# Layer 1's memory projections behind the modulation, other places for weight halves, and unread transposes of the identity on TensorE

## The chip, the cores and the metric

The kernel runs on one core of a Trainium2 chip. What is measured is the device time of one execution in microseconds (us). A core has five engines that run side by side, each with its own queue of instructions in a fixed order: TensorE (PE; its weight loads are listed apart, as PEld), VectorE (DVE), ScalarE (ACT), GpSimd (POOL) and SyncE (SP), which here issues the transfers from memory. An instruction waits on semaphores for its inputs and for free buffers, and everything behind it on its engine waits with it.

## The reference

One sequence of 256 tokens, 1024 wide, in float32, goes through two blocks.

The first block has two layers. For each, `mod = silu(c) @ ada_w[layer] + ada_b[layer]` gives six rows (shift, scale and gate, twice), and then

```python
h = rms_norm(x, norm1_g) * (1 + sc1) + sh1
x = x + g1 * mixer(h)                  # layer 0: retention and attention; layer 1: stick-breaking
h = rms_norm(x, norm2_g) * (1 + sc2) + sh2
x = x + g2 * grouped_moe(h, ...)       # 16 experts, two for each token
```

`grouped_moe` takes a sigmoid score of each token for each expert, picks the best of four groups of experts, two experts in it, and adds their SwiGLU results with the scores as weights.

The second block has two layers too: half a feed-forward network, a mixer (layer 0: the RWKV scan; layer 1: dilated attention on shared keys and values) and another half network. Both mixers also attend to a memory of 256 rows, `mem`, whose keys and values for layer l are `rms_norm(mem, mem_norm[l]) @ mem_w_kv[l]`, with a norm on each head of the keys.

## The kernel before

**Layout and products.** The tokens stand transposed, `xT` [128, 8, 256]: eight tiles of 128 features by 256 tokens. Weights come in pieces of [128, 2048], 1 MB each, by SyncE's transfers (L300 and the loads beside it), into a few rooms that are used in turn. For most products each operand is split into a rounded part (`wh`, `xh`, by ScalarE, L350) and a remainder (`wl`, `xl`, by VectorE or GpSimd, L351), and TensorE multiplies three pairs (`mm3`). Every matmul is recorded at L330 and every transpose by the identity at L346. A transpose of the identity itself gives nothing that is used; such an instruction is called a turn here, as is any use of `tr`.

**What sets the order.** The program is written as one sequence, function after function. A planner then orders the instructions of each engine: of those that are ready by its own modelled durations it takes the one that the program has first. `tc.issue_after(instruction)` holds what stands under it until that instruction has been issued. RWKV_ORDER (L203) and B_ORDER (L204) are orders of steps written out by hand. Buffers with a tag (`self.t`, `self.ps` for the banks in which matmuls accumulate) are used in turn, so an instruction can also wait for a room.

**Start.** `first_layer` (L1149) for layer 0 first calls `mem_kv` (L1243): the memory is loaded (one transfer), its squares are summed (`prep`, `step`, `fin`), it is scaled by each layer's norm gain, and the keys and values for both layers are projected, 32 matmuls for each of the keys and values of a layer. Then the modulation rows are made from `ada` weights (1 MB each), the norm of x is finished (`fin`, L411: a reciprocal root, two transposes that spread it to `rB`), and `modulated` (L427) makes the mixer's input. For each of eight tiles VectorE multiplies by `rB`, multiplies by the gain and adds the shift, and subtracts the rounded part that ScalarE makes. The first weight of the mixer is split ahead of all that, by `ws` (L309).

**Layer 1's entry.** The same `fin` and `modulated` run once layer 0's experts have been added to x.

**Routing and experts.** `residual` (L462) adds the mixer's output to x. `route` (L815) makes the routing logits: eight matmuls of a broadcast shift, then the token's own, on a bank `g`. `moe` (L1061) turns the input (sixteen transposes, `hY`), waits for VectorE to pick the experts, and gathers the tokens of each by matmuls with one-hot matrices (`gather`, 32 for a pair of experts). The experts are done in eight blocks of two experts by 64 tokens (a block that depends on the data follows for more tokens). `hidden` (L1013) and `down` (L1033) run the matmuls of the two experts in turn, expert 0 on the upper 64 columns of TensorE and expert 1 on the lower, each with its own weight piece: four halves of gate and up and two of down in a block. `scatter` (L1055) adds the results into four banks; at the end VectorE adds these to x and the next norm's sums are taken.

**The second block.** `rwkv` (L1283, its loop over RWKV_ORDER at L1579) and `b_mixer` (L1601, loop at L1621) run the steps of the two mixers; the feed-forward networks are before and after them.

Of the kernel before, what the change touches and what calls it, by code (L numbers as in the profile page):

```python
# [199 lines left out]
F32R = mybir.dt.float32r  # L200
RWKV_LANES = 3
RWKV_BANKS = dict(pp=1, g0=(1, 1), g1=(1, 1), l0=2, l1=2, l2=2)
RWKV_ORDER = "M s0 M M M s1 s2 p0 s3 m0 p1 s4 s5 p2 m1 s6 m2 s7 s8 p3 p4 s9 a3 a0 m3 m4 a1 p5 m5"  # L203
B_ORDER = "n q2 n q1 q2 M0 q0 q1 M1 q0 P1 P0"  # L204
B_OUT = 1, 0
B_BANKS = dict(pp=2, tn=1, a0=2, a1=2, x=1)
SHARED_ORDER = "012345"
# [33 lines left out]
class Net:  # L241
# [67 lines left out]
    def ws(self, name, i):  # L309

        if (name, i, "split") in self.ahead:
            return self.ahead.pop((name, i, "split"))
        t = self.ahead.pop((name, i), None)
        if t is None:
            t = self.raw(name, i)
        o = []
        for h in range(2):
            hi, lo = (self.tile([128, 1024], n, F32R, 3) for n in ("wh", "wl"))
            self.split(t[:, 1024 * h:1024 * h + 1024], hi, lo, self.lo_engines[self.nlo % len(self.lo_engines)])
            self.nlo += 1  # L320
            o.append((hi, lo))
        return o

    def v(self, name):
        s, w = VEC[name]
# [17 lines left out]

    def tr(self, out, x):
        p = x.shape[0]
        self.nc.tensor.transpose(out, x, self.ident[:p, :p])  # L346

    def split(self, src, hi, lo, eng=None):

# [74 lines left out]
        st.rB = self.tile([128, 256], "rB", bufs=2)  # L424
        nc.scalar.activation(st.rB, p.rearrange("p t z -> p (t z)"), AF.Copy)

    def modulated(self, st, gain, shift):  # L427

        nc = self.nc
        x = self.xtiles()  # L430
# [31 lines left out]
    def residual(self, name, mix, chunks, banks, after, gate=None):  # L462

        xT = self.xT
        p = [self.ps(b, [128, 2, 256]) for b in banks]
        n = len(chunks)
        for i, c in enumerate(chunks):
            w = self.ws(name, c)
            if i < n - 1:
                order = [(h, d) for h in range(2) for d in range(8)]  # L470
            else:
                order = [(h, d) for d in (0, 2, 4, 6, 1, 3, 5, 7) for h in range(2)]
            for h, d in order:
                self.mm3(p[d // 2][:, d % 2], [y[:, d * 128:d * 128 + 128] for y in w[h]], mix[2 * c + h],
                         i == h == 0 and d % 2 == 0, i == n - 1 and h == 1)
# [339 lines left out]
    def route(self, st, gain, shift):  # L815
# [197 lines left out]
    def hidden(self, xg, wsrc):  # L1013

        nc = self.nc
        V = nc.vector
        gu = []
        for nm in ("eg", "eu"):
            p = self.ps("g")
            for h in range(2):  # L1020
                w = [wsrc(nm, e, h) for e in range(2)]
                for k in range(4):
                    for e in range(2):
                        kk = 4 * h + k
                        self.mm(p[64 * e:64 * e + 64], xg[kk][:, 64 * e:64 * e + 64], w[e](k), kk == 0, kk == 7)
            gu.append(p)
        th = self.t("th", [128, 512])
        nc.scalar.activation(th, gu[0], AF.Tanh, scale=0.5)
        V.scalar_tensor_tensor(th, th, 1.0, gu[0], op0=OP.add, op1=OP.mult)
        V.tensor_tensor(th, th, gu[1], op=OP.mult)  # L1030
        return th

    def down(self, th, wsrc, wc):  # L1033

        nc = self.nc
        V = nc.vector
        p = self.ps("x", [128, 4, 128])
        for f in range(4):
            self.tr(p[:, f], th[:, f * 128:f * 128 + 128])
        hT = self.t("heT", [128, 4, 128])  # L1040
        nc.scalar.activation(hT, p, AF.Copy)
        out = []
        for n in range(2):
            w = [wsrc("ed", e, n) for e in range(2)]
            p = self.ps("g")
            for f in range(4):
                for e in range(2):
                    self.mm(p[64 * e:64 * e + 64], hT[:, f, 64 * e:64 * e + 64], w[e](f), f == 0, f == 3)
            hi, lo = self.t("yh", [128, 512], F32R), self.t("yl", [128, 512], F32R)
            nc.scalar.activation(hi, p, AF.Copy, scale=wc)  # L1050
            V.scalar_tensor_tensor(lo, p, wc, hi.bitcast(F32), op0=OP.mult, op1=OP.subtract)  # L1051
            out.append((hi, lo))
        return out

    def scatter(self, y, sc, acc, first, last):  # L1055
        for d in range(8):
            c = d % 4 * 128
            for part in range(2):
                self.mm(acc[d // 2][:, d % 2], y[d // 4][part][:, c:c + 128], sc, first and d % 2 == part == 0, last and part == 1)

    def moe(self, l, st, after, ahead):  # L1061
        nc = self.nc
# [6 lines left out]
        for t in range(2):  # L1069
            h = []  # L1070
            for half in range(2):
                p = self.ps("acc", [128, 512])
                with self.tc.issue_after(st.last.ins):
                    for k in range(4):
                        self.tr(p[:, 128 * k:128 * k + 128], xT[:, 4 * half + k, t * 128:t * 128 + 128])
# [66 lines left out]
        self.wturn = 0  # L1142
        for key in ahead:
            self.ahead[key] = self.raw(*key)
        for d in range(8):
            V.scalar_tensor_tensor(xT[:, d], acc[d // 2][:, d % 2], gate[:, d:d + 1], xT[:, d], op0=OP.mult, op1=OP.add)
            after(d)

    def first_layer(self, l, st, nxt):  # L1149
        nc = self.nc  # L1150
        xT = self.xT
        if l == 0:
            self.use(A=dict(cb=4, dec=2, rope=1, rq=1, rk=1, rv=1, rg=1, av=2, hn=2, hsq=1, q=2, k=2, sT=2, Pa0=1, Pa1=1, PTa0=1, PTa1=1,
                            me0=(4, 4), me1=(8, 4), me2=(18, 4), me3=(22, 4)),
                     B=dict(ra=2, rb=2, nx=8), C=dict(oa0=1, oa1=1), P=EVEN_BANKS)
            self.mem_kv()
            for k in range(0, 8, 2):
                nc.sync.dma_start(xT[:, k:k + 2], self.a["xT"].rearrange("p (k t) -> p k t", k=8)[:, k:k + 2])
            for d in range(8):
# [5 lines left out]
                     C=dict(neg1=1, one=1, never=1),  # L1165
                     P=ODD_BANKS)
        st = st()
        self.fin(st, "tn" if l == 0 else "o")
        V, P = self.nc.vector, self.nc.gpsimd
        self.lo_engines = [dict(V=V, P=P)[c] for c in LO_FIRST[l]]  # L1170
        key = (("even_i", dict(g0=8, g1=11, h0=0, h1=1)[EVEN_ORDER[:2]]), ("odd_i", 0))[l]
        self.ahead[(*key, "split")] = self.ws(*key)
        x = self.modulated(st, self.mod_gain(l, 1, self.v(f"n1_{l}")), self.mod[l][:, 0:8])
        mix = self.mixed()
        if l == 0:
            jobs = iter(ADA0)
# [63 lines left out]
            V.scalar_tensor_tensor(xT[:, d], p[:, 0], 0.25, xT[:, d], op0=OP.mult, op1=OP.add)  # L1240
            after(d)

    def mem_kv(self):  # L1243

        nc = self.nc
        mT, other = (self.tile([128, 8, 256], n) for n in ("ml", "mh"))
        self.load(mT, self.a["memT"].rearrange("p (k t) -> p k t", k=8))
        ws = [[self.wload(self.a[f"memkv{l}"][i], f"me{2 * l + i}") for i in range(2)] for l in range(2)]
        st = self.prep("ad", late=7)
        for d in range(8):  # L1250
            self.step(st, d, mT[:, d])
            for l, to in enumerate((other, mT)):
                nc.scalar.activation(to[:, d], mT[:, d], AF.Copy, scale=self.v(f"memn{l}")[:, d:d + 1])
        st = st()
        self.fin(st, "ad", False)
        self.kv = self.tile([128, 2, 4, 256], "kv")
        for l, x in enumerate((other, mT)):
            ps = []
            for i, w in enumerate(ws[l]):
                p = self.ps(f"a{i}", [128, 2, 256])  # L1260
                for t in range(2):
                    for k in range(8):
                        self.mm(p[:, t], x[:, k, t * 128:t * 128 + 128], w(k // 2)[:, k % 2 * 256:k % 2 * 256 + 256], t == k == 0, k == 7)
                ps.append(p)
            kT, v = self.kv[:, l, :2], self.kv[:, l, 2:]
            k = self.head_norm(ps[0], st.r)
            for t in range(2):
                nc.scalar.activation(v[:, t], ps[1][:, t], AF.Copy, scale=st.r[:, t:t + 1])
            self.memory[l] = kT, v
            self.channels(k, self.v(f"memk{l}"), kT)  # L1270

    def gain8(self, name):
        g = self.t("g8", [128, 1])
# [9 lines left out]
    def rwkv(self, st, mix, partial, memory, tags):  # L1283
# [317 lines left out]
    def b_mixer(self, st, dkv, kv, after):  # L1601
# [17 lines left out]
        q = [o[:, i] for o in o3 for i in range(2)]  # L1619
        normed = {}  # L1620
        for what in B_ORDER.split():  # L1621
            if what[0] in "nq":
                c = 0 if what == "n" else 1 + int(what[1])
                if c not in normed:
# [104 lines left out]
```

## Time and profile before

| | |
|---|---|
| median of the runs | 2148.67 us (2148.67, 2152.56, 2137.82) |
| the profiled execution | 2150.5 us, its span 2148.7 us |
| mean granted clock of TensorE | 0.965 of full |
| busy: PE | 2025.2 us (94% of the span) |
| busy: PEld | 1517.2 us |
| busy: DVE | 1143.9 us |
| busy: ACT | 854.1 us |
| busy: POOL | 478.9 us |
| transfers | 481.71 MB, 224 GB/s on average |

The span is the time from the first to the last instruction of the profiled execution; what lies around it is 1.8 us. TensorE's busy share is over the whole span and holds stretches of different kinds. All times below count from the span's start. In rows, `p<-wh,B` reads: into a bank `p` from the tiles `wh` and `B` by the program's names; PEclk is the clock that TensorE was granted in the stretch, 1.00 for 2.4 GHz and 0.50 for 1.2 GHz. The stages in order: memory and modulation to 67 us, the even mixer to 223, routing to 247, layer 0's experts to 535, the entry of layer 1 to 555, the odd mixer to 702, routing to 722, layer 1's experts to 975, then the second block with the scan mixer from 1170 and the last mixer from 1866 us.

### The profile page before, as it was taken

What the parts mean: (1) busy time and instruction counts of PE and PEld (TensorE: products, weight loads), DVE (VectorE), ACT (ScalarE), POOL (GpSimd) and SP (SyncE); (2) the same over time, 40 slices, a digit from 0 to 9 for tenths busy, and PEclk for the clock granted to TensorE, in tenths of its full rate; (3) what the DMA queues carried; (4) which work ended last, traced back from release to release, by engine and by line L of the source; (5) the groups of instructions that cost most, each with busy time, mean ns of one, the idle gap of its engine ahead of it and who ended that gap; (6) DMA issues with size and microseconds to landing.
All of it is one profiled execution on the core that took longest, in us unless ns stands there. A gap on an engine that the chain in (4) does not pass through costs nothing.

```text
span 2148.7 us, 32734 instructions
## 1 busy us (share of the span) xinstructions
PE 2025.2 (94%) x12766; PEld 1517.2 (71%) x12766; DVE 1143.9 (53%) x2331; ACT 854.1 (40%) x1566; POOL 478.9 (22%) x501
## 2 busy tenths in 40 slices
PE   8999999689899999799999899989999999899999
PEld 6778644233767544337888787768889888888887
DVE  2756511121533511207776778767767676746774
ACT  3443311102444321015554434335555555445652
POOL 1001100000000100003533443225523453422540
PEclk9999899999899999999999999989999999988999
DMA  9779599879377599793552221025555555512553
GB/s 373 290 262 367 210 421 425 354 313 391 123 282 275 226 416 424 308 416 138 186 187 98 106 83 44 21 83 192 185 188 176 177 195 180 204 59 98 195 183 114
DMA packets 80899, 481.71 MB, mean 224 GB/s; under 512 B 8800, under 2 KB 12384, under 8 KB 29792
## 3 DMA queue, kind: packets, MB, share of 16 engines
q1 hardware_dynamic: 80736, 479.52, 58.4%
q8 instruction: 105, 1.72, 0.3%
q14 instruction: 58, 0.48, 0.1%
HBM read 478.43 MB, written 1.05 MB: 223 GB/s over the span
## 4 chain that ended last, share of the span: by engine, by line
PE 51%; DVE 5%; issue 1%; ACT 1%; POOL 1%; DMA 0%; DVEq 0%; ACTq 0%; POOLq 0%
PE p L330 50%; PE p L346 1%; DVE wl L351 1%; DVE s_hsum L522 0%; DVE A L1430 0%; DVE B L1403 0%; DMA w<-a_o 0%; DVE A L1481 0%; ACT wh L350 0%; POOL acc L401 0%; DVE s_hsum L514 0%; DVE w L1503 0%; DVE s_rs_oh L361 0%; DVE C L1555 0%; DVE s_rs_th L362 0%
## 5 line engine op out<-in xcount | busy, mean ns | idle before, releaser
L351 DVE TENSOR_TENSOR wl<-w,wh 128x1024 fp32r<-128x1024 f32 x352 | 454.0, 1291 | 223.0 <-ACT wh L350 219.9
L350 ACT ACTIVATE wh<-w 128x1024 fp32r<-128x1024 f32 x384 | 404.8, 1057 | 347.9 <-PE p L330 321.8
L330 PE MATMUL p<-xh,wh 128*128 128x512 f32 (+1 forms) x1056 | 328.3, 366 | 10.2 <-ACT xh L350 4.1
L330 PE MATMUL p<-xl,wh 128*128 128x512 f32 (+1 forms) x1056 | 320.1, 359 | 0.0
L330 PE MATMUL p<-xh,wl 128*128 128x256 f32 x880 | 251.4, 286 | 1.2 <-DVE wl L351 1.2
L330 PE MATMUL p<-xl,wl 128*128 128x256 f32 x880 | 248.8, 283 | 0.0
L330 PEld LDWEIGHTS p<-xh,wh 128*128 128x128 f32 x1056 | 191.5, 193 | 50.1 <-issue 5.9
L330 PEld LDWEIGHTS p<-xl,wh 128*128 128x128 f32 x1056 | 187.0, 188 | 37.1 <-issue 5.5
L330 PEld LDWEIGHTS p<-xh,wl 128*128 128x128 f32 x880 | 168.0, 191 | 3.1 <-DVE wl L351 1.6
L330 PEld LDWEIGHTS p<-xl,wl 128*128 128x128 f32 x880 | 165.1, 188 | 1.8 <-issue 1.4
L330 PE MATMUL p<-A,wh 128*128 128x512 f32 x448 | 159.4, 397 | 0.0
L401 POOL TENSOR_TENSOR acc<-acc,sq 128x256 f32<-128x256 f32 x44 | 44.0, 1000 | 409.3 <-ACT sq L396 407.8
L330 PEld LDWEIGHTS p<-B,A 128*128 128x128 f32 x706 | 92.2, 196 | 60.9 <-issue 39.5
L330 PE MATMUL p<-A,wl 128*128 128x256 f32 x448 | 125.8, 281 | 0.0
L330 PE MATMUL p<-B,A 128*128 128x256 f32 (+1 forms) x706 | 114.4, 305 | 9.5 <-DVE A L1051 2.3
L351 POOL TENSOR_TENSOR A<-B,A 128x256 fp32r<-128x256 f32 x56 | 82.8, 1478 | 140.3 <-ACT A L350 140.1
L1051 DVE SCALAR_TENSOR_TENSOR A<-p,s_wc,A 128x512 fp32r<-128x512 f32 x34 | 25.5, 751 | 157.7 <-ACT A L1050 146.9
L330 PE MATMUL p<-w,B 128*64 128x512 f32 x256 | 109.1, 616 | 0.0
L330 PE MATMUL p<-wh,B 128*128 128x256 f32 (+1 forms) x312 | 96.8, 417 | 11.6 <-PEq L1133 11.6
L330 PE MATMUL p<-A,A 64*64 64x64 f32 (+8 forms) x868 | 102.1, 286 | 5.0 <-DVE A L1541 3.0
L330 PEld LDWEIGHTS p<-A,wh 128*128 128x128 f32 x448 | 84.2, 188 | 20.3
L351 POOL TENSOR_TENSOR wl<-w,wh 128x1024 fp32r<-128x1024 f32 x32 | 77.4, 2417 | 90.9 <-ACT wh L350 90.7
(459 smaller groups left out, 3991.3 us busy)
## 6 DMA issues: line engine op xcount, KB each, us to landing
w<-fprei SPq DMA_DIRECT2D x44, 1024.0 KB, 4.8
w<-fposti SPq DMA_DIRECT2D x44, 1024.0 KB, 4.8
wa<-ada SPq DMA_DIRECT2D x42, 1024.0 KB, 6.4
w<-ed SPq DMA_DIRECT2D x24, 1024.0 KB, 12.8
w<-eg SPq DMA_DIRECT2D x22, 1024.0 KB, 13.4
w<-fpreo SPq DMA_DIRECT2D x22, 1024.0 KB, 4.8
w<-fposto SPq DMA_DIRECT2D x22, 1024.0 KB, 4.8
wa<-ed SPq DMA_DIRECT2D x16, 1024.0 KB, 12.6
```

The lines of the kernel that those rows point to most:

```text
L330: return self.nc.tensor.matmul(out, lhsT, rhs, start=start, stop=stop, skip_group_check=True, **k)
L346: self.nc.tensor.transpose(out, x, self.ident[:p, :p])
L350: self.nc.scalar.activation(hi, src, AF.Copy)
L351: (eng or self.nc.vector).tensor_tensor(lo, src, hi.bitcast(F32), op=OP.subtract)
L401: nc.gpsimd.tensor_tensor(st.acc, st.acc, sq, op=OP.add)
L1051: V.scalar_tensor_tensor(lo, p, wc, hi.bitcast(F32), op0=OP.mult, op1=OP.subtract)
```

## The change

It has four parts.

1. `mem_kv` is cut in two: `mem_load` (the loads, the squares and the scaling; the memory comes in four transfers, not one) and `mem_kv(l)`. Layer 0's part stands where both stood; layer 1's part comes after `modulated`. The memory's norm is finished behind layer 0's projections.
2. `modulated` splits the two halves of the mixer's first weight behind tiles 0 and 3, not ahead of all. In layer 0 the eight multiplications by `rB` stand ahead of the rest. In layer 1 a tile takes two three-operand instructions on VectorE and one on ScalarE between them, which adds the shift as a bias.
3. Turns that nobody reads (`warm`) stand at eight places: 6 in `route`, behind the residual's last matmul, and 14 in `moe`, behind the turns of the input (both in both layers); 6 in `moe` behind the last `scatter` (both layers); 6 and 10 around layer 1's `fin`; 8 in `rwkv` ("W" in its order) and 12 in `b_mixer`.
4. In `hidden` and `down` the matmul of expert 1 comes ahead of that of expert 0.

```diff
-RWKV_ORDER = "M s0 M M M s1 s2 p0 ...
-B_ORDER = "n q2 n q1 q2 M0 q0 q1 M1 q0 P1 P0"
+RWKV_ORDER = "M s0 W M M M s1 s2 p0 ...
+B_ORDER = "n q2 W n q1 q2 M0 q0 q1 M1 q0 P1 P0"
...
+    def warm(self, n, bank):
+        p = self.ps(bank, [128, 128]) if isinstance(bank, str) else bank
+        for _ in range(n):
+            self.tr(p, self.ident)
...
-    def modulated(self, st, gain, shift):
+    def modulated(self, st, gain, shift, key, early):
         x = self.xtiles()
+        halves = self.halves(*key)
+        o = []
+        ts = []
+        for k in range(8):
+            ts.append(self.t("nx", [128, 256]))
+            if early:
+                V.tensor_tensor(ts[k], self.xT[:, k], st.rB, op=OP.mult)
         for k in range(8):
             hi, lo = x[k]
-            t = self.t("nx", [128, 256])
-            nc.vector.tensor_tensor(t, self.xT[:, k], st.rB, op=OP.mult)
-            nc.vector.tensor_scalar(t, t, gain[:, k:k + 1], shift[:, k:k + 1], op0=OP.mult, op1=OP.add)
-            self.split(t, hi, lo)
+            t = ts[k]
+            if early:
+                V.tensor_scalar(t, t, gain[:, k:k + 1], shift[:, k:k + 1], op0=OP.mult, op1=OP.add)
+                self.split(t, hi, lo)
+            else:
+                V.scalar_tensor_tensor(t, self.xT[:, k], gain[:, k:k + 1], st.rB, op0=OP.mult, op1=OP.mult)
+                nc.scalar.activation(hi, t, AF.Identity, bias=shift[:, k:k + 1])
+                V.scalar_tensor_tensor(lo, t, shift[:, k:k + 1], hi.bitcast(F32), op0=OP.add, op1=OP.subtract)
+            if k in (0, 3):
+                o.append(next(halves))
+        self.ahead[(*key, "split")] = o
         return x
...
     # route
-        p = self.ps("g", [128, 16])
+        p = self.ps("g")
+        with self.tc.issue_after(self.last.ins):
+            self.warm(6, p[:, 128:256])
+        p = p[:, :16]
...
     # hidden and down
-                    for e in range(2):
+                    for e in (1, 0):
...
     # moe, behind the sixteen turns of the input
+        with self.tc.issue_after(turn.ins):
+            self.warm(14, "x")
...
     # moe, behind the last scatter
+        with self.tc.issue_after(self.last.ins):
+            self.warm(6, "x")
...
     # first_layer
-            self.mem_kv()
+            self.mem_load()
+            self.mem_kv(0)
...
-        self.fin(st, "tn" if l == 0 else "o")
+        for n in (6, 10):
+            if l:
+                with self.tc.issue_after(st.last.ins):
+                    self.warm(n, "o")
+            self.fin(st, "tn" if l == 0 else "o")
...
-        self.ahead[(*key, "split")] = self.ws(*key)
-        x = self.modulated(st, self.mod_gain(l, 1, self.v(f"n1_{l}")), self.mod[l][:, 0:8])
+        x = self.modulated(st, self.mod_gain(l, 1, self.v(f"n1_{l}")), self.mod[l][:, 0:8], key, l == 0)
+        if l == 0:
+            self.mem_kv(1)
...
-    def mem_kv(self):
+    def mem_load(self):
-        self.load(mT, self.a["memT"].rearrange("p (k t) -> p k t", k=8))
+        for k in range(0, 8, 2):
+            self.load(mT[:, k:k + 2], self.a["memT"].rearrange("p (k t) -> p k t", k=8)[:, k:k + 2])
...
+    def mem_kv(self, l):
+        st, xs, ws = self.mem
+        x = xs[l]
...
+        if l == 0:
+            self.fin(st, "ad", False)
...
     # rwkv ("l2", 8) and b_mixer ("x", 12)
+            if what == "W":
+                with self.tc.issue_after(self.last.ins):
+                    self.warm(8, "l2")
+                continue
```

`halves` is the loop of `ws` as a generator: it makes one half of a weight's split each time it is asked. `fin` returns at once when the norm's row is there, so its second call in layer 1 does nothing.

## Rows read from the trace of the kernel before

**Rows 1.** Stretches: from:to, length, busy (x instructions) PE PEld DVE ACT POOL, PEclk, DMA, GB/s
```profile
66.60:223.30 156.70, 156.51 (x1232) 128.55 (x1229) 93.59 (x223) 62.94 (x111) 11.86 (x14) 1.00 0.81 307
...
974.80:982.20 7.40, 5.50 (x19) 4.82 (x19) 6.72 (x12) 5.05 (x11) 0.00 (x0) 0.54 0.31 102
...
1180.20:1187.00 6.80, 3.91 (x20) 3.86 (x20) 4.42 (x14) 0.81 (x2) 1.94 (x3) 0.75 0.41 154
...
1871.90:1883.30 11.40, 5.33 (x26) 5.33 (x26) 9.14 (x31) 2.23 (x3) 3.13 (x2) 0.70 0.26 93
```

**Rows 2.** Order in time of the start: start, length, engine, line, tiles, count, idle before
```profile
25.28 4.13 SPq L300 DMA_DIRECT2D w<-ada  x3
...
31.72 5.78 PE L330 MATMUL p<-A,ml 128*128 128x256 f32 x26
...
37.77 8.37 PE L330 MATMUL p<-A,ml 128*128 128x256 f32 x38
...
54.74 1.91 PE L330 MATMUL p<-w,cact 128*32 128x512 f32 x12
...
58.67 2.77 DVE L434 TENSOR_TENSOR B<-xT,rB 128x256 f32<-128x256 f32 x8 [0.25 <-ACT rB L425]
...
62.99 3.64 PE L330 MATMUL p<-wa,cact 128*32 128x512 f32 x16
...
72.45 0.60 ACT L512 ACTIVATE A<-p 128x512 f32<-128x512 f32 x1 [1.60 <-PE p L330]
```

**Rows 3.** Transfers of the first 62 us: count, size, median us from issue to landing
```profile
w<-ada SPq DMA_DIRECT2D x3, 1024.0 KB, 12.9
```

**Rows 4.** Four turns in the order of time; two stretches in layer 1's routing, in turn
```profile
37.33 0.60 PE L346 MATMUL p<-cm,A 128*128 128x128 f32 x4
...
709.10:712.40 3.30, 3.30 (x16) 3.22 (x16) 2.60 (x17) 2.53 (x5) 0.61 (x3) 0.50 0.77 308
712.50:715.80 3.30, 0.36 (x6) 0.17 (x4) 2.53 (x14) 2.20 (x5) 0.11 (x1) 1.00 0.00 0
```

**Rows 5.** Order in time at the routings, in an expert block, and an expert load
```profile
227.32 6.15 PE L330 MATMUL p<-C,xT 128*128 128x16 f32 x30
...
233.31 3.65 PE L346 MATMUL p<-cm,xT 128*128 128x128 f32 x16
...
240.81 5.73 PE L330 MATMUL p<-B,A 128*128 128x128 f32 x32 [0.71 <-DVE B L955]
...
258.46 0.33 SPq L300 DMA_DIRECT2D xl<-eg  x1
...
452.63 2.00 PE L330 MATMUL p<-B,A 128*128 128x128 f32 x16
...
716.33 5.22 PE L330 MATMUL p<-B,A 128*128 128x128 f32 x32 [0.70 <-DVE B L955]
```

**Rows 6.** Layer 1's entry: order in time, stretches, and two VectorE groups (min/median/max ns)
```profile
541.60 0.38 ACT L425 ACTIVATE rB<-p 128x256 f32<-128x256 f32 x1 [4.81 <-PE p L346]
...
547.29 2.35 DVE L351 TENSOR_TENSOR wl<-w,wh 128x1024 fp32r<-128x1024 f32 x2
...
542.00:550.00 8.00, 1.16 (x2) 0.58 (x2) 7.98 (x20) 5.49 (x11) 0.00 (x0) 0.50 0.00 0
550.00:555.30 5.30, 5.28 (x24) 5.28 (x25) 3.45 (x8) 0.00 (x0) 0.00 (x0) 0.50 0.55 198
555.50:558.20 2.70, 2.70 (x25) 2.70 (x24) 1.23 (x1) 0.89 (x1) 0.00 (x0) 1.00 0.00 0
...
L434 DVE TENSOR_TENSOR B<-xT,rB x16: 414/417/425, 58.7 to 544.4; 128x256 f32<-128x256 f32 x16
...
L1146 DVE SCALAR_TENSOR_TENSOR xT<-p,mod,xT x16: 473/476/484, 528.1 to 976.1; 128x256 f32<-128x256 f32 x16
```

**Rows 7.** An expert block's order in time; SyncE's waits, 262 to 378 us (us, count, longest)
```profile
335.12 1.02 PE L330 MATMUL p<-wh,B 128*64 128x512 f32 x2
...
SPq L300 <- PE p L330: 30.0, 15, 6.3
```

More of the change, by code (lines that the diff above doesn't have):

```diff
@@ L312, in ws, with halves @@
             return self.ahead.pop((name, i, "split"))
+        return list(self.halves(name, i))
+    def halves(self, name, i):
         t = self.ahead.pop((name, i), None)
@@ L315, in ws @@
             t = self.raw(name, i)
-        o = []
         for h in range(2):
@@ L320, in ws @@
             self.nlo += 1
-            o.append((hi, lo))
-        return o
+            yield hi, lo
     def v(self, name):
@@ L345, in tr @@
         p = x.shape[0]
-        self.nc.tensor.transpose(out, x, self.ident[:p, :p])
+        return self.nc.tensor.transpose(out, x, self.ident[:p, :p])
+    def warm(self, n, bank):
+        p = self.ps(bank, [128, 128]) if isinstance(bank, str) else bank
+        for _ in range(n):
+            self.tr(p, self.ident)
     def split(self, src, hi, lo, eng=None):
@@ L473, in residual @@
             for h, d in order:
-                self.mm3(p[d // 2][:, d % 2], [y[:, d * 128:d * 128 + 128] for y in w[h]], mix[2 * c + h],
-                         i == h == 0 and d % 2 == 0, i == n - 1 and h == 1)
+                self.last = self.mm3(p[d // 2][:, d % 2], [y[:, d * 128:d * 128 + 128] for y in w[h]], mix[2 * c + h],
+                                     i == h == 0 and d % 2 == 0, i == n - 1 and h == 1)
                 if i == n - 1 and h == 1:
@@ L1046, in down @@
             for f in range(4):
-                for e in range(2):
+                for e in (1, 0):
                     self.mm(p[64 * e:64 * e + 64], hT[:, f, 64 * e:64 * e + 64], w[e](f), f == 0, f == 3)
@@ L1058, in scatter @@
             for part in range(2):
-                self.mm(acc[d // 2][:, d % 2], y[d // 4][part][:, c:c + 128], sc, first and d % 2 == part == 0, last and part == 1)
+                self.last = self.mm(acc[d // 2][:, d % 2], y[d // 4][part][:, c:c + 128], sc, first and d % 2 == part == 0, last and part == 1)
     def moe(self, l, st, after, ahead):
@@ L1074, in moe @@
                     for k in range(4):
-                        self.tr(p[:, 128 * k:128 * k + 128], xT[:, 4 * half + k, t * 128:t * 128 + 128])
+                        turn = self.tr(p[:, 128 * k:128 * k + 128], xT[:, 4 * half + k, t * 128:t * 128 + 128])
                 h.append(self.t("hY", [128, 512]))
@@ L1253, in mem_kv @@
                 nc.scalar.activation(to[:, d], mT[:, d], AF.Copy, scale=self.v(f"memn{l}")[:, d:d + 1])
-        st = st()
-        self.fin(st, "ad", False)
         self.kv = self.tile([128, 2, 4, 256], "kv")
[L1257 to L1266, printed above, removed]
-            for t in range(2):
-                nc.scalar.activation(v[:, t], ps[1][:, t], AF.Copy, scale=st.r[:, t:t + 1])
-            self.memory[l] = kT, v
-            self.channels(k, self.v(f"memk{l}"), kT)
+        self.mem = st(), (other, mT), ws
+    def mem_kv(self, l):
+        st, xs, ws = self.mem
+        x = xs[l]
+        ps = []
+        for i, w in enumerate(ws[l]):
+            p = self.ps(f"a{i}", [128, 2, 256])
+            for t in range(2):
+                for k in range(8):
+                    self.mm(p[:, t], x[:, k, t * 128:t * 128 + 128], w(k // 2)[:, k % 2 * 256:k % 2 * 256 + 256], t == k == 0, k == 7)
+            ps.append(p)
+        if l == 0:
+            self.fin(st, "ad", False)
+        kT, v = self.kv[:, l, :2], self.kv[:, l, 2:]
+        k = self.head_norm(ps[0], st.r)
+        for t in range(2):
+            self.nc.scalar.activation(v[:, t], ps[1][:, t], AF.Copy, scale=st.r[:, t:t + 1])
+        self.memory[l] = kT, v
+        self.channels(k, self.v(f"memk{l}"), kT)
     def gain8(self, name):
@@ L1621, in b_mixer @@
         for what in B_ORDER.split():
+            if what == "W":
+                with self.tc.issue_after(self.last.ins):
+                    self.warm(12, "x")
+                continue
             if what[0] in "nq":
```

3 lines of the change are left out of this document (2 added, 1 removed).

## The prediction

> **What bounds the kernel now.** I began with the table of stretches [rows 1]: which engine fills each stretch, and at which clock TensorE ran. A reader should see two kinds of stretch. Between 66.6 and 223.3 us TensorE is busy 156.5 of 156.7 us at full clock, so whatever reaches that stretch earlier is earlier at its end. The three other rows are waits between stages: TensorE is granted 0.54 to 0.75 of its clock there, having had little to do, and its first work after the wait runs at 1.2 instead of 2.4 GHz. The start, both routings and layer 1's entry are of the same kind [rows 2, 4 to 6]. Then I read the order in time around each of these places, for what ends the wait.
>
> At the start [rows 2] the two halves of the memory's keys and values are projected before anything else: layer 1's 64 matmuls hold TensorE from 31.72 to 46.14. The modulation's matmuls, whose last three weights were issued by 29.41 and land 12.9 us after issue [rows 3], so by 42.3, therefore end at 56.65, and the normalised input can only be scaled from 58.67. The first projection's result is read at 72.45.
>
> **Part 1, layer 1's memory moved.** Its 64 matmuls cost 14.4 us (5.78 + 8.37 and the gap for four turns) wherever they stand. In front of the modulation they delay it; behind, the modulation waits for its weights alone: 42.3, half a microsecond for the last matmuls, and the 2.0 us that lay between 56.65 and 58.67, so scaling begins at 44.8 instead of 58.67. If the planner puts nothing of the memory into the wait for weights, TensorE does the 14.4 us from 43.3 to 57.7, the first projection to 63.0 (48 matmuls at 0.108, [rows 6]) and the 16 modulation matmuls that it had already done before (3.64 at the half clock, 1.9 at the full one [rows 2]) to 65: 7.4 earlier than 72.4. If it fills the wait, all that is left at 31.5 (14.4; 64 modulation matmuls at 0.12, between 0.114 and the 0.159 of 12 in 1.91, 7.7; 5.2; 1.9) ends at 60.7: 11.7 earlier. VectorE isn't in the way: the eight multiplications by the norm (2.77) come before the modulation now, and two operations of that price for each of eight tiles plus two weight halves (16 x 0.346 + 2.35 [rows 6]) end near 53. The loads stay in their order; memT in four pieces adds three issues to SP's queue (0.33 each by the nearest row of one [rows 5]) in front of the memory weights, and lets the first square start when a quarter has landed, which counts only if the wait is filled: I allow 2.4 for it at the upper end, a fifth of the 12.9. The late norm statistics of the memory move behind matmuls that wait for nothing of it: nothing, with the projections as cover. Lower end: the planner leaves the order as it is, and only the 2.77 of multiplications go: 3. Upper end 14 (11.7 + 2.4). I take the middle of the two orders, **9.5**, and it passes whole through the stretch that TensorE fills.
>
> **Part 2, turns at the routing, both layers.** Six turns stand between the residual's last matmul and the routing's. TensorE goes from the one to the other without idle time (the row at 227.32 has none before it [rows 5]), so they are on the path: four turns of this kind took 0.60 [rows 4], 0.11 each behind the first, so 0.65 a layer, a loss of 1.3. The 30 routing matmuls have one to sixteen columns and ran at half clock (6.15 us); I do not expect six turns to hold the clock through them. Fourteen turns follow the sixteen turns of the input, in the wait for VectorE's choice of experts. That wait covers them: the sixteen end at 236.96, the gather starts at 240.81, and fourteen at half clock last 3.2. They should let the clock rise before the gather. Its 32 matmuls took 5.73 and 5.22, and sixteen of that shape at full clock 2.00 [rows 5], so 4.0 for 32: 1.7 + 1.2 won. The first expert load that waits for a room goes out at 258.46, after TensorE's first experts, so this gain reaches the expert stage. Net **1.6**; ends -1.3 (turns cost and hold nothing) and 7.7 (the 30 matmuls at full clock too, half of 6.15 less, in both layers).
>
> This rests on turns counting as work for the clock. In layer 1 they did: from 709.1 to 712.4 TensorE did nothing but 16 turns at clock 0.50, and the next stretch, with six matmuls in it, was granted 1.00 [rows 4]. The Trainium skill (TensorE: Matmul & The Clock Gate, Part 4, PE-mode transpose) says the opposite, that the full clock "doesn't engage for transpose-mode". By it, every gain of clock in parts 2 to 4 would go; this trace speaks against it, once.
>
> **Part 3, entry of layer 1.** Now [rows 6]: the norm row is ready at 541.98, VectorE works 7.98 of the next 8.00 us (eight multiplications, eight scalings, two weight halves, first remainders), and TensorE's steady flow begins at 550.02, at half clock (24 matmuls in 5.30) until 555.4. After: per tile one operation on VectorE, one on ScalarE, one on VectorE, and the weight halves behind tiles 0 and 3. A three-operand operation lasts 0.476 alone, and I take 0.42 a piece in sequence (the same ratio as 0.417 alone to 0.346 in sequence for the multiplications): 16 x 0.42 + 2.35 = 9.1, the last tile at 551.1, not 552.5; but the first tile and weight half (two pieces of 0.42, ScalarE's between them, half of the 2.35) are ready after some 2.6, at 544.6. From there 48 matmuls at half clock end at 555.1; with the clock up, the last 15 end 1.7 after the last tile, at 552.8. So 3.3 to 5.6; **4**. The ten turns wait for the bank that ScalarE frees at 541.98 and end by 544.2, just before the first matmul; six more lie in VectorE's chain for the norm. Ends 2 (the weight halves' remainders ahead of the tiles in VectorE's queue) and 6.
>
> **Part 4, the other turns.** Six at the end of layer 1's experts, eight in the scan block, twelve in the last mixer. The half clock costs there at most half of what TensorE did in the stretch, 5.50, 3.91 and 5.33 [rows 1], so 7.4 in all. The turns fill 0.65, 0.9 and 1.3 us of 1.9, 2.9 and 6.1 of idle time (stretch less busy), a fifth to a third; I take a third of the 7.4: **2.5**. No engine waits for them, and their banks have no reader: cost nothing, with the wait as cover; ends 0 and 7.4.
>
> **Part 5, second expert first.** Same matmuls. TensorE's queue does not move past a weight that hasn't landed. With the first expert ahead, its two instructions can run while the second's weight is on its way; with the second ahead, everything waits. Where no wait is real, the planner's split (two matmuls alone for 1.02, then other work [rows 7], six such in layer 0's fixed blocks) goes away: half of it each at most, 6 us for both layers. Where each of the 96 groups (two layers, eight blocks, four halves of gate and up and two of down) lost as much, 49. Between, SP waits 30.0 us for TensorE on these rooms in layer 0 [rows 7], so mostly the weights are early: I take **0**.
>
> **Sum.** 9.5 + 1.6 + 4 + 2.5 = 17.6. The profiled execution took 2150.5 us (its span 2148.7), 1.8 above the median of 2148.67: 2150.5 - 17.6 = **2133**.
>
> **Rivals.**
> *Everything lands.* The wait is filled and memory starts sooner (14), the clock holds at the routing (7.7), at layer 1 (6) and at the other waits (7.4): 35.1, so 2115. For it: half-clock rows at every one of these places. Against: the waits are longer than the turns.
> *Turns hold nothing* (the page's rule, as a mechanism here: each wait ends at half clock as now, and the gathers stay at 5.73 and 5.22): 9.5 + 3 (order alone in part 3) - 1.3 = 11.2, so 2139. Against it the one rise after sixteen turns.
> *The move isn't one.* The planner, which sees modelled weights arrive late, still sends layer 1's memory first: part 1 gives 3, total 11.1, so 2139. Against: it placed ready work by the order of the program elsewhere, as the 16 matmuls at 62.99 in the wait for scaling.
> *Slower: the second expert's weight is what TensorE waits for.* Place: the 96 groups of the two expert stages. Price 0.51 a group, 49 in all, so 2150.5 - 17.6 + 49 = 2182. It decides from 0.18 a group upwards (17.6 / 96), that is, if the weight is late in about a third of them. Against: SP waiting for TensorE.
>
> **Numbers.** Chances: forecast 0.47 (own range 2124 to 2142), everything 0.24, turns hold nothing 0.13, no move 0.08, slower 0.08. Range 2112 to 2152: from some way below the best case to just above no gain, with the slow case and a tenth of scatter left out. A measurement tells about 1% from no change, so faster means under 2127 and slower above 2170. Faster 0.40 (the 0.24 and a third of the forecast's 0.47), same 0.52, slower 0.08.
>
> **What would show it.** Right: scaling of tile 0 near 45 to 50 and the first attention's head norm read at 61 to 65; gathers of 4 us at clock 1.00; the first projection of layer 1 read 3 to 5 us after less of a wait, counted from its norm row; no DMA among TensorE's waits in the expert blocks. Wrong: the modulation's sum near 55 or later; a gather above 5 us; TensorE waiting for expert weights before a second expert's matmul; or stages that aren't touched, the four feed-forward networks above all, of another length.

## The result and the profile after

The changed kernel takes 2119.98 us (median of four runs, 2108.61 to 2124.88) where the kernel before takes 2148.39: 0.9885 of it, 95% interval 0.9847 to 0.9923. A second series of six runs gave 0.9871 [0.9840, 0.9903]. The time lies inside the forecast's wide range (2112 to 2152) and below its own range (2124 to 2142, around 2133); several of its terms did not come. The profiled execution took 2124.88 us, its span 2123.1 (before 2148.7).

Where the 25.6 us between the two spans lie is read by the same instruction in both traces, stage by stage (differences of two starts; the first is counted from the span's start):

| from, to | before | after | difference |
|---|---|---|---|
| start, last matmul of layer 0's residual | 223.26 | 219.25 | -4.0 |
| routing, to the first expert matmul | 23.21 | 23.72 | +0.5 |
| experts of layer 0, first to last matmul | 284.94 | 282.35 | -2.6 |
| entry of layer 1, to the first projection's reading | 26.98 | 22.39 | -4.6 |
| mixer of layer 1, to its residual's last matmul | 143.06 | 139.20 | -3.9 |
| routing of layer 1 | 20.01 | 23.82 | +3.8 |
| experts of layer 1 | 250.20 | 238.52 | -11.7 |
| entry of the second block, to its 61st matmul | 20.22 | 18.77 | -1.4 |
| the rest: the last mixer -3.0, what follows it +1.3 | | | -1.7 |

The largest row is one that the forecast put at nothing, and in this trace both routings became longer. First the stretches of after that answer to [rows 1]: from, to, length, busy time of PE, PEld, DVE, ACT and POOL, PEclk, DMA share, GB/s.

```profile
66.00:219.20 153.20, 152.51 (x1201) 123.49 (x1200) 90.58 (x220) 61.52 (x109) 11.91 (x14) 1.00 0.84 315
952.20:959.00 6.80, 4.48 (x31) 3.88 (x30) 6.80 (x12) 5.70 (x12) 0.00 (x0) 1.00 0.18 37
1156.00:1163.00 7.00, 4.87 (x29) 4.63 (x29) 4.69 (x14) 0.81 (x2) 2.21 (x3) 0.76 0.40 150
1847.70:1859.10 11.40, 6.64 (x38) 6.40 (x38) 9.36 (x31) 2.24 (x3) 3.35 (x2) 0.70 0.26 93
```

Of the three waits of part 4, one now has the full clock (0.54 before, 1.00 after); the scan's has 0.76 (0.75 before) and the last mixer's 0.70 as before. At the first of them the other traces agree: the eleven with turns have at most 3.4 us at half clock there, the three without 6.8 to 10.2. Next the start of after, in order of time (start, length, engine, line, tiles, count, idle before), beside [rows 2]:

```profile
43.46 3.29 PE L331 MATMUL p<-A,ml 128*128 128x256 f32 x14
...
52.25 1.06 PE L331 MATMUL p<-w,cact 128*32 128x512 f32 x8
...
55.15 2.67 DVE L451 TENSOR_SCALAR B<-B,s_mg,mod 128x256 f32<-128x256 f32 x8
...
56.06 0.38 PE L331 MATMUL p<-wh,xh 128*128 128x256 f32 x1 [1.37 <-ACT xh L357]
...
58.21 0.79 PE L331 MATMUL p<-wh,xh 128*128 128x256 f32 x2 [1.65 <-DVE xh L358]
...
66.29 1.92 PE L331 MATMUL p<-wa,cact 128*32 128x512 f32 x16
```

The modulation's last weight landed at 42.68, as forecast. But the planner mixed the memory's matmuls with the modulation's, also behind that landing: the modulation's last eight stand at 52.25, behind memory matmuls such as the fourteen at 43.46. So the scaling begins at 55.15 and not near 45. By then no memory matmul is left to cover it: TensorE waits twice (1.37 and 1.65 us), and its projection runs at half clock to 63.7.

The entry of layer 1 in after, beside [rows 6]:

```profile
533.72 0.38 ACT L432 ACTIVATE rB<-p 128x256 f32<-128x256 f32 x1 [1.46 <-PE p L347]
...
534.16 1.86 PE L347 MATMUL p<-cm 128*128 128x128 f32 x10 [0.47 <-ACT rB L432]
...
535.46 3.25 DVE L454 SCALAR_TENSOR_TENSOR B<-xT,s_mg,rB 128x256 f32<-128x256 f32 x8
...
537.26 3.64 PE L331 MATMUL p<-wa,cact 128*32 128x512 f32 x16
540.83 0.58 PE L331 MATMUL p<-xh,wh 128*128 128x256 f32 x1
```

From the norm's row (534.10) to the steady flow (540.83) are 6.7 us, 8.0 before; and 3.64 of these hold sixteen modulation matmuls which before stood in the mixer, on its path. From the norm's row to the first projection's reading are 13.6 us, 16.4 before, a gain of 2.8. The other 1.8 of the entry's 4.6 lie ahead of the row: before, sixteen matmuls of the norm's sums ran at half clock, 3.58 us from 535.27; after, 1.95 from 529.22. The row comes as early after the last expert matmul in the kernel without any turn, so the turns are not what gives these 1.8.

The routing of layer 1, in route_x's and route22's forms too, is shown with the experiments.

### The profile page after: what moved, and what is told of

Same layout as the page of the kernel before. It is cut to its first block, busy times and chain, and to the rows that moved or that the text cites. A ratio compares the mean times of both kernels' runs of the same rounds, so it can differ in the third digit from the quotient of the medians.

```text
span 2123.1 us, 32887 instructions
## 1 busy us (share of the span) xinstructions
PE 2006.3 (94%) x12854; PEld 1515.6 (71%) x12854; DVE 1144.2 (54%) x2323; ACT 855.8 (40%) x1566; POOL 478.8 (23%) x501
## 4 chain that ended last, share of the span: by engine, by line
PE 50%; DVE 6%; issue 1%; ACT 1%; POOL 1%; DMA 0%; DVEq 0%; POOLq 0%; ACTq 0%
PE p L331 49%; PE p L347 1%; DVE wl L358 1%; DVE s_hsum L545 0%; DVE A L1472 0%; DVE s_rs_th L369 0%; DVE B L1445 0%; DMA w<-a_o 0%; DVE s_rs_oh L548 0%; DVE A L1523 0%; DVE w L1545 0%; ACT wh L357 0%; POOL acc L408 0%; DVE s_hsum L537 0%; DVE w L1507 0%
## 5 line engine op out<-in xcount | busy, mean ns | idle before, releaser
L331 PE MATMUL p<-A,A 64*64 64x64 f32 (+7 forms) x868 | 103.1, 288 | 5.0 <-DVE A L1583 3.0
L331 PEld LDWEIGHTS p<-A,A 128*64 128x64 f32 (+3 forms) x868 | 77.3, 171 | 26.1 <-issue 6.9
```

The lines of the kernel that those rows point to most:

```text
L331: return self.nc.tensor.matmul(out, lhsT, rhs, start=start, stop=stop, skip_group_check=True, **k)
```

## The experiments

Ratios are to the kernel before, on the same chip; each experiment is an edit of the whole change unless it says otherwise.

| kernel | median us | before | ratio, 95% interval |
|---|---|---|---|
| whole | 2116.54 | 2140.47 | 0.9871 [0.9840, 0.9903] |
| no_move | 2123.38 | 2139.48 | 0.9912 [0.9882, 0.9943] |
| no_turns | 2121.62 | 2139.48 | 0.9905 [0.9878, 0.9932] |
| first_first | 2132.53 | 2139.48 | 0.9952 [0.9931, 0.9973] |
| old_entry | 2120.62 | 2139.48 | 0.9905 [0.9873, 0.9937] |
| hold | 2129.07 | 2140.47 | 0.9929 [0.9902, 0.9955] |
| no_route | 2127.06 | 2140.47 | 0.9918 [0.9888, 0.9948] |
| before_exp | 2135.49 | 2140.47 | 0.9967 [0.9944, 0.9990] |
| route22 | 2111.44 | 2146.08 | 0.9855 [0.9821, 0.9890] |
| route_x | 2109.39 | 2146.08 | 0.9843 [0.9808, 0.9878] |
| steady | 2121.55 | 2146.08 | 0.9886 [0.9855, 0.9917] |
| both | 2120.06 | 2146.08 | 0.9879 [0.9847, 0.9911] |

An interval is 9 to 15 us wide, so of the parts only the experts' order shows in the times alone; the others are read from the traces. Two traces of the changed kernel itself (after and whole) differ by up to 2.5 us in one stage, which is the size that a single trace can tell.

**whole**, the changed kernel beside the others.

> The whole change again, beside the other kernels on one chip: the reference for the parts. From the traces so far, 0.9885 of the kernel before, and as in the others the last mixer runs either wholly at the full clock or with some 24 us at the half one, which is 9.4 us (the step at 1920 us between the profiles).

It came out so, 0.9871; its trace has the 24 us at half clock in the last mixer, as after has.

**first_first**: the experts' order undone.

```diff
-                    for e in (1, 0):
+                    for e in range(2):
```

> All of the change but the order of experts: the first expert's matmul is ahead of the second's again. Theory: in layer 1 the expert stage of after is 11 us shorter than before, 4 of it in the fixed blocks, where the pairs of matmuls that stood alone (0.91 us for two) are gone; layer 0's is about 1 shorter. If the order of experts does that, this kernel takes 2127 to 2132 us and the stage of layer 1 is 254 us again. Rival (the prediction's part 5): the order is worth nothing, and the 11 us are differences between executions in the blocks that depend on the data: 2120.

0.9952, its interval apart from that of whole: undoing the order takes back most of the gain. Its layer 1 experts take 247.78 us (238.52 after). The lines in order of time show how. An expert's matmul uses 64 of TensorE's columns, and two of them, one of each half, run side by side: starts 0.01 us apart, one such pair every 0.43. In before, where the first expert led:

```profile
815.94 1.07 PE L330 MATMUL p<-ml,B 128*64 128x512 f32 x2
816.94 1.09 PE L330 MATMUL p<-B,A 128*128 128x256 f32 x7
817.97 0.64 PE L330 MATMUL p<-xl,B 128*64 128x512 f32 x1
817.97 0.64 PE L330 MATMUL p<-ml,B 128*64 128x512 f32 x1
...
825.70 1.02 PE L330 MATMUL p<-wa,B 128*64 128x512 f32 x2
```

and in after:

```profile
801.37 0.64 PE L331 MATMUL p<-mh,B 128*64 128x512 f32 x1
801.37 0.64 PE L331 MATMUL p<-wh,B 128*64 128x512 f32 x1
801.85 0.59 PE L331 MATMUL p<-mh,B 128*64 128x512 f32 x1
801.85 0.59 PE L331 MATMUL p<-wh,B 128*64 128x512 f32 x1
```

A matmul is here a record of the trace, and the trace has two for each of these matmuls of the program: 48 in a block of two experts, nine blocks in layer 0 (eight fixed, one that depends on the data) and eight in layer 1 are 816, and there are 1632 records. So the two at 815.94 are one matmul of the program. Before, the planner sent two matmuls of the first expert's weight (`ml`) ahead, other work behind them, and from then on each pair joined matmuls of neighbouring groups, until two were left alone at the end (825.70). Of 1632 such matmuls 104 stand alone before, 52 in each layer, 98 in first_first, none in after. Two alone take two slots in place of one: 52 x 0.43 = 22 us of TensorE's time, 11 in each layer.

**before_exp**: the kernel before with this order alone.

> The kernel before, with the second expert's matmul ahead of the first's and nothing else of the change. Theory: before, 104 of the experts' 1632 half-wide matmuls run alone, in pairs of two slots of 0.43 us; after none does. Without them 52 x 0.43 = 22 us of TensorE's time go, of which the undoing showed 11 to 13 on the path: 2127 us where before takes 2139.5, and no matmul alone. Rival: the parts depend on each other (the order gains only behind the other edits): under 5.

2135.49, 0.9967 [0.9944, 0.9990]: a gain, but the expected 2127 of 2139.5 (0.9942) lies just outside the interval. By the medians the order is worth 5 us here and 16 between first_first and whole; the traces' 14 lie between the two. Eight matmuls still stand alone in this kernel, four in each layer, and layer 1's experts take 239.22 us, so the 11 us of that stage come with the order alone. All twelve traces with the new order have 236.8 to 239.2 there. Layer 0's stage is less clear: 279.9 to 284.8 in the twelve, 284.9 in both traces with the old order. Where the same slots go in the two layers is seen in the ends of the blocks (lengths in us, from the stage's first matmul or the end before, 96 matmuls to a block; in brackets the matmuls alone before):

| | first five blocks, before and after | the block that depends on the data | last three blocks |
|---|---|---|---|
| layer 0 | 146.1, 142.2 (20) | 45.8, 51.4 (12) | 93.0, 88.7 (20) |
| layer 1 | 149.0, 142.2 (28) | none | 101.2, 96.3 (24) |

In the fixed blocks of both layers the lost slots are the time: half of 40 matmuls at 0.43 are 8.6 us in layer 0, and 8.2 are won; half of 52 are 11.2 in layer 1, and 11.7 are won. What differs is the block that depends on the data, which this input has in layer 0 alone. TensorE waits there for the block's own weights, 12.1 us in all before:

```profile
402.63 1.94 PE L330 MATMUL p<-mh,B 128*64 128x512 f32 x2 [6.96 <-DMA mh<-eg]
404.98 1.12 PE L330 MATMUL p<-ml,B 128*64 128x512 f32 x1 [0.41 <-DMA ml<-eg]
```

and 17.0 after:

```profile
400.77 1.09 PE L331 MATMUL p<-ml,B 128*64 128x512 f32 x1 [12.42 <-DMA ml<-eg]
```

The second expert's first weight (`ml`) lands 158.5 us behind the stage's first matmul before and 157.7 after, so what the blocks in front of it have won is waited away.

**no_move**: the memory as before.

```diff
             self.mem_kv(0)
+            self.mem_kv(1)
...
-        if l == 0:
-            self.mem_kv(1)
```

> All of the change but the move: layer 1's memory projections stand directly behind layer 0's, ahead of the modulation. Theory (the traces of before and after, read against each other): the move is worth 4.2 us, because the work that TensorE has done by 72.45 us before is done by 68.14 after; so some 2124 us, and the first result of the mixer's projections is read some 4 us later than after. Rival (the prediction's part 1): the move is worth 9.5 and something else gave 5 back: 2129.5.

The first projection is read at 71.65 us (66.40 after, 72.45 before). The stages of layer 0's mixer stand 3.2 us later than in after, and 2.3 later than in whole, all the way to the experts: the move is worth 2 to 4, not 9.5.

**hold**: layer 1's memory waits for the modulation.

```diff
+            with self.tc.issue_after(self.modulation.ins):
-            self.mem_kv(1)
+                self.mem_kv(1)
```

`self.modulation` keeps the last matmul of the modulation.

> The whole change, and layer 1's memory projections wait until the modulation's last matmul has been issued. Theory: in after the planner laid memory matmuls between the modulation's (14, 6 and 8 of them among the last 24), whose last ended at 53.3 although its weight was there by about 43; TensorE then stood still for 2.8 us and ran at half clock to 63.7. Held back, the modulation ends near 43.5, the 14.4 us of memory cover the scaling, and the work that ends at 68.14 in after ends near 65: 3 us less. Rival: TensorE waits from 33 to 43 for weights with nothing to do, and that costs what the cover gives: 0 or some us more.

The rival won. The first projection is read at 69.21 (66.40 in after). In order of time:

```profile
45.71 1.94 PE L331 MATMUL p<-w,cact 128*32 128x512 f32 x8 [0.47 <-DMA w<-ada]
47.58 5.75 PE L331 MATMUL p<-A,ml 128*128 128x256 f32 x20
53.16 0.60 PE L347 MATMUL p<-cm,BX 128*128 128x128 f32 x4
53.60 9.66 PE L331 MATMUL p<-A,ml 128*128 128x256 f32 x44
62.91 0.47 PE L331 MATMUL p<-wh,xh 128*128 128x256 f32 x1
```

The last weight lands at 45.67, three us later than in after (42.68). It was issued 1.5 us later and took 15.0 us to land, not 13.5. TensorE waits for it, drops to half clock, and twenty memory matmuls get in front of the four turns of the modulation, so the scaling starts at 54.22, 0.9 earlier than in after. Layer 0's residual ends at 222.29, where no_move has it (222.46) and 3.0 later than after: in this trace nothing of the move's gain is left. How much of that is the order and how much the late weight stays open.

**old_entry**: layer 1 scaled as before.

```diff
+        if not early:
+            for k in range(8):
+                ...
+                V.tensor_tensor(t, self.xT[:, k], st.rB, op=OP.mult)
+                V.tensor_scalar(t, t, gain[:, k:k + 1], shift[:, k:k + 1], op0=OP.mult, op1=OP.add)
+                self.split(t, hi, lo)
+            return x
```

> All of the change but layer 1's way of scaling its input: the weight halves first, then three VectorE operations a tile. The turns stay. Theory: from the norm's row (ScalarE, 541.98 before, 534.1 after) to the flow of matmuls took 8.0 us before and 2.4 after (matmuls at 536.5), of which the way of scaling is 3 to 4: some 2123 to 2124 us. Rival: the turns' clock does it, and the way of scaling less than 1: 2120.

The entry takes 24.13 us; 22.39 and 21.53 with the new way (after, whole), 22.55 with it and no turns. In nine traces with the new way it is 21.3 to 22.6; two have 24.2 and 24.4, one with the old order of experts (first_first) and one whose norm row comes 3 us later (hold). So the scaling is worth 1.6 to 2.9 of the entry's gain, and the turns there less than a trace can tell.

**no_turns**: no turn at any place.

```diff
         for _ in range(n):
-            self.tr(p, self.ident)
+            return
```

> All of the change but the turns: none of the eight places has any. Theory: the turns give 1.5 us at the entry of the second block (the stages of after start 1.5 earlier there, at full clock), about 2 to 3 at layer 1's entry, and cost 0.8 at each routing, whose gather stayed at the half clock: together 2 to 3, so 2122 to 2123 us. Rival: the clock that they hold is the larger part of the gain of 28, 10 or more: 2130 or later. Second rival (turns hold nothing): 2118, as they only cost.

0.9905, an interval that meets that of whole. The entry of the second block takes 25.03 us (18.7 to 22.3 in the eleven traces with turns, 20.22 before), the scan's entry 1.5 less than in after, as it does in steady, which has the scan's turns; layer 1's routing 20.02 in place of 23.82. The turns give at one place what they cost at another, and the times don't tell the sum from nothing.

**no_route**, without the turns at the routing; **route22**, without the six and with 22 for 14; **route_x**, the six in a bank of their own:

```diff
-            self.warm(6, p[:, 128:256])
+            self.warm(6, "x")
```

> The whole change without the 6 and 14 turns at the two routings. Theory: they hold nothing (the gather took 5.44 us in both layers after, 5.73 and 5.22 before) and stand on the path: 0.8 a layer back, up to 2.4 in layer 1 (the step of the kernel without any turns): 2 to 3 us less than the whole change. Rival: their clock is worth as much as they cost: no difference.

> The whole change without the 6 turns in front of the routing's matmuls, and with 22 in the wait for the choice of experts instead of 14 (14 end 0.9 us before the next matmul and the gather starts 2 us after them). Theory: with 14 the gather ran at full clock in most profiles (3.74 us), but the clock fell in front of it in some (5.37); without them it takes 5.2 to 6.1; the 22 reach up to it, so 3.7 in both layers. Without the 6, layer 1's sixteen shift matmuls go back to where they stood before, inside the mixer's waits: from the last matmul of the residual to the first expert matmul 20 us in layer 1 (22.3 without turns, 23.1 to 26.1 with all). Together 2 to 4 us less than the whole change. Rival: the falls come from elsewhere and the gather stays mixed: 1 us less at most.

> The whole change, with the 6 turns at the routing in a bank of their own (x) and not in the bank of the shift matmuls. Theory: what the six cost in layer 1 is not their 0.8 us but that the sixteen shift matmuls (1.86 us), which use the same bank, must stand behind them; in another bank these stand early again and layer 1's stretch is 1.9 us shorter than in after, the logits' one 0.8 longer than without turns. Rival: the planner leaves the shift matmuls late anyway: no difference.

From the residual's last matmul to the first expert matmul, and for layer 1 (whose shift matmuls can stand on either side of that mark) also from the first projection's reading:

| kernel | layer 0 | layer 1 | layer 1 from the reading |
|---|---|---|---|
| before | 23.21 | 20.01 | 163.08 |
| no_turns, no_route | 23.21, 23.21 | 20.02, 20.03 | 160.05, 160.49 |
| after, whole | 23.72, 22.28 | 23.82, 21.37 | 163.02, 160.45 |
| route_x | 22.37 | 20.15 | 160.46 |
| route22, both | 21.25, 21.24 | 18.45, 18.10 | 158.89, 158.55 |

The sixteen shift matmuls of layer 1 stand behind the residual in after and whole, and inside the mixer before and in no_route, route_x and route22. So the six turns pulled them along through the shared bank, as expected. What that costs is less than the expected 1.9: inside the mixer they are on TensorE's path too, 1.2 us of it (139.1 to 140.4 from the reading to the residual's last matmul), and counted from the reading whole and route_x agree (160.45, 160.46). In after the stretch is longer than in whole by its gather (below) and its logits: with the six turns in front the logits of layer 1 take 4.9 to 6.4 us, without them 4.0 to 4.9.

The 14 turns do what the forecast expected of them, if one looks at the stretch that they lead to. The turns of the input and the gather without turns between them (no_route, stretches as above):

```profile
693.20:696.90 3.70, 3.63 (x17) 3.23 (x17) 2.82 (x19) 2.79 (x6) 0.61 (x3) 0.50 0.91 365
700.60:706.60 6.00, 6.00 (x34) 5.88 (x34) 4.72 (x21) 1.50 (x4) 0.00 (x0) 0.61 0.14 30
```

and with 22 (route22):

```profile
692.30:695.70 3.40, 3.40 (x17) 3.40 (x18) 2.61 (x17) 2.51 (x5) 0.62 (x3) 0.50 0.83 317
699.70:703.40 3.70, 3.70 (x32) 3.58 (x32) 3.41 (x12) 1.45 (x4) 0.00 (x0) 1.00 0.00 0
```

All 20 gathers of the ten kernels with turns there start at full clock, all 8 of the four without start at the half. With 14 the clock fell again just behind the gather's start in 5 of 16 (5.44 us in place of 3.81), in after in both layers. With 22 it held in all four, which is too few to tell from 11 of 16. Nor does the length of the gap show that the turns must reach up to the gather: the next matmul comes 0.94 to 1.02 us behind the turns in the five that fell, and 0.18 to 1.36 in the eleven that held. After, layer 0, and then route22, layer 1:

```profile
233.57 2.10 PE L347 MATMUL p<-cm 128*128 128x128 f32 x14
236.61 0.28 PE L331 MATMUL p<-C,C 128*128 128x16 bf16 x5 [0.94 <-DVE C L910]
237.60 5.44 PE L331 MATMUL p<-B,A 128*128 128x128 f32 x32 [0.71 <-DVE B L981]
...
695.70 2.79 PE L347 MATMUL p<-cm 128*128 128x128 f32 x22
698.69 0.27 PE L331 MATMUL p<-C,C 128*128 128x16 bf16 x5 [0.20 <-DVE C L908]
699.66 3.81 PE L331 MATMUL p<-B,A 128*128 128x128 f32 x32 [0.70 <-DVE B L979]
```

**steady**, eight turns more in each of two waits of the last mixer, and **both**, with route22's edit:

```diff
+            if steady:
+                with self.tc.issue_after(score.ins):
+                    self.warm(steady, "x")
```

> The whole change, and eight turns more behind the scores of each of two attention steps of the last mixer, in front of the wait (1.04 us, then 0.63) in which the clock fell for 23.9 us in half of the profiles, before and after, at a cost of 9.4 us. Theory: the fall begins in that wait, when TensorE's few matmuls leave it idle; with turns in it the stretch stays at full clock in every execution: the slower half of the whole change's times (2121 to 2126 beside 2108 to 2112) goes, median 2110 or a little above. Rival: the fall starts elsewhere (the matmuls of 64 columns themselves); the times keep their two groups and the turns cost up to 2.

> The two edits together: 22 turns at the routing and none in front of it, and the eight turns in the last mixer's waits. If both theories hold: 2106 to 2110 where before takes 2140, and no two groups of times. If neither: as the whole change, 2117.

A miss. The clock still fell in that mixer, for 13.6 us in steady's trace and 27.3 in both's; the times lie from 2114.86 to 2122.53 and from 2113.75 to 2124.45. The turns also shifted the planner's order there, so it is not shown that the fall has another cause, only that these turns don't hold it off. Of the kernels tried, route_x and route22 have the lowest medians, 0.9843 and 0.9855 of before; their intervals overlap those of the changed kernel.

## Why the prediction was right or wrong

- **Part 1** (9.5) was mis-sized: 4.0. The weights landed as forecast (42.68, 42.3). What failed is the filled order, in which TensorE goes from the memory through the modulation to the projection without a gap. The planner laid memory matmuls between the modulation's last ones, which end at 53.3, and had none left for the scaling, so TensorE waited 3.0 us and did most of the projection at half clock.
- **Part 2** (gain 1.6) had its two halves right and missed a third. The clock rises and the gather runs in 3.81 us (forecast 4.0), in 15 of 20; that the turns use the bank of the shift matmuls was in the diff and wasn't followed, though those stand elsewhere in layer 1. In after it lost 0.5 and, net of the mixer's 1.2, 2.6; in whole it won 0.9 and lost 0.2.
- **Part 3** (4) is 4.6 at the entry, inside its ends, but 2.8 in the stretch that its sum is about, behind the norm's row; that the row itself came 1.8 earlier was no part of it. Of the mixer's 3.9, 1.2 belongs to the shift matmuls of part 2, and about 1.9 to sixteen modulation matmuls that now fill the entry's wait. They do so in before_exp too (at 538.8 us), and not in first_first, so that comes with the order of experts and not with this part.
- **Part 4** (2.5) is 1.4 at one of its three places in after, where the eleven traces with turns scatter by 3.6, and nothing at the scan. The last mixer's first wait ends as late as before, at the same 0.70.
- **Part 5** (0) is the step that failed: 11.7 in layer 1, 2.6 in layer 0. Two errors. It counted six splits from rows that show two matmuls alone in one line; the trace has 104 matmuls alone, and the ends of the chains stand in other rows. And it read "SyncE waits 30 us for TensorE" [rows 7] as a reason for nothing; early weights mean that TensorE sets the pace, and in the fixed blocks its lost slots were the time (8.2 won of 8.6 in layer 0, 11.7 of 11.2 in layer 1). Layer 0 gave 5.6 back in the block that depends on the data. The rival in which the second expert's weight makes TensorE wait fell in the fixed blocks: no transfer stands among TensorE's waits there in after. In the block that depends on the data it is what TensorE waits for (12.42 us), but that block ends 191.3 to 196.1 us behind the stage's first matmul with the new order and at 191.2 and 191.9 with the old one, so it costs between nothing and 5 once.
- **The page's rule**: the Trainium skill (TensorE: Matmul & The Clock Gate, Part 4, PE-mode transpose) says that the full clock doesn't engage for transposes. The gathers above speak against it: 20 of 20 start at full clock behind unread turns, none of 8 without. The trace lists the turns as matmuls and doesn't show whether they run in the mode that the page means. So "turns hold nothing" falls at the gather, and at the second block's entry too.

Two of the forecast's own signs of being wrong came in after: the modulation's sum at 54.73, and gathers of 5.44. The sum came out within its range because part 5's 14.3 took the place of what parts 1, 2 and 4 did not give. That the time fits is luck; the reasons were half right.

## What to carry to other kernels

Where two half-wide matmuls share TensorE, look in the order of time for ones that start alone, at both ends of a chain, and price them by the slot; then look for a place further on where TensorE waits for a transfer, since what was won is waited away there. Filler that shares a buffer with real work takes that work along; give it a buffer of its own. Whether it must reach up to the work that it is for is not shown here. A queue that waits for the engine says that the engine is the bound.

## What the runs showed of the hardware

Six of the fourteen traces, those of before and after among them, have 23.9 us at half clock in the second half of the last mixer; most others have none or 3.4 there. In after (columns as above):

```profile
1891.00:1921.00 30.00, 28.33 (x123) 23.14 (x124) 12.76 (x29) 12.19 (x27) 0.00 (x0) 0.60 0.03 10
```

and where it stays up, in hold:

```profile
1895.00:1920.00 25.00, 22.02 (x150) 17.39 (x149) 13.31 (x31) 12.67 (x29) 0.00 (x0) 1.00 0.05 21
```

Between such traces the stages behind it move by 9.4 us, while most other stages of one kernel agree to 2.5. That is about half of the spread of the changed kernel's times (2108 to 2126), and more than any part of the change but the experts' order. What decides it stays open.
